# A matmul with rotary embedding on one core: which rows of x share a partition, and which queue brings the block pairs

## The chip, the cores and the metric

The kernel runs on one core of one Trainium2 chip. The metric is the device time of one execution in microseconds, the median over several executions.

## The reference

x has 16 images of 512 rows and 768 columns, in fp32. Each row is multiplied by a 768 x 768 weight, and the 768 results, taken as 12 heads of 64, are rotated by cos and sin, which depend on the row's place in its image alone:

```
y = np.matmul(x, weight)                       # (16, 512, 768) @ (768, 768)
y = y.reshape(batch, seq, n_heads, head_dim)   # 12 heads of 64
y1, y2 = y[..., :32], y[..., 32:]
out1 = y1 * cos1 - y2 * sin1                   # cos, sin: (512, 64), by row of the image
out2 = y2 * cos2 + y1 * sin2
out = np.concatenate([out1, out2], axis=-1)    # fp32, (16, 512, 768)
```

## The kernel before

**Tiles and groups.** The 8192 rows are cut into 64 tiles of 128 rows, and four tiles make a group (16 groups, `QB = 4`). Partition p of a tile holds row 4p + r of one image; a group has the same r in four images (`where`, line 192). So all columns of a group use the same cos and sin rows. Two tiles side by side are a pair; group g has pairs (g, 0) and (g, 1). An image row in DRAM has 3 KB.

**A normal tile.** SyncE loads it as fp32 (`load`, line 206, buffers xs). ScalarE casts it to fp16 and brings its columns into another order (`cast`, line 241, buffers xc). TensorE turns it in PSUM (`turn`, and from tile 4 to 60 `turn_rows`, line 261, which turns the two halves of 64 rows at the same time: line 271 in the profile). ScalarE copies the turned tile to SBUF (buffers xt). These copies and casts all run through the helper `copy`, line 190.

**A block pair.** The second pair of groups 5 to 13 and of group 15 (`BLOCKS`) is not turned by TensorE. It comes in four DMAs of 32 partitions, one per quarter of the columns (`load_quarter`, line 214, packets of 768 bytes), so that VectorE's transpose of 32 x 32 blocks (`turn_pair`, line 287, a STREAM_TRANSPOSE at line 299) finishes the turn. Six pairs come from SyncE as fp32 (buffers xb) and are cast by ScalarE (`cast_pair`, line 279, buffers xd). Four pairs (groups 6, 8, 10, 12) come from GpSimd's queue, whose DMA casts them to fp16 on the way (buffers xh), and need no cast on an engine.

**Matmul and rotation.** From tile 4 on, two streams of matmuls run on the two row halves of TensorE, the second 1024 columns behind the first (`walk`, `one`, `both`; line 362). Six PSUM banks hold a group's 3072 result columns, in units of 512 or 1024. For each unit VectorE multiplies the PSUM columns by cos and by sin (`rope`, line 396; one TENSOR_TENSOR at line 419 writes both products), and GpSimd adds the two products, the second with its half heads exchanged (line 445), into buffers ov. They are stored 768 KB at a time (`store`, line 467), mostly from ScalarE's queue. In the last group some adds are made by TensorE and VectorE.

**Order.** Every engine works through its instructions in the order in which the program issues them, and `Flow.do` puts a semaphore wait ahead of an instruction that needs another engine's result. The order is written out by hand in the main loop over tiles i (line 668). At the end of step i it issues, in this order, the turn of tile i + 3 (with ScalarE's copy), then ScalarE's casts up to tile i + 5, then GpSimd's loads and the stores:

```
700  turns(i + 1 + (T_AHEAD if i > QB else 2), 1)           # T_AHEAD = 3
701  casts(i + 1 + (C_AHEAD if i > QB else 4), 1 + i % 2)   # C_AHEAD = 5
702  pool_loads(i + P_AHEAD)
```

`casts` walks over the tiles; at a normal tile it calls `castx` (line 553), at the first tile of a block pair `cast_pair`, and after each it calls `pump` (line 517), which issues the next loads of the list `fetch` as long as buffers are free (NX tiles, NB block pairs).

Of the kernel before, what the change touches and what calls it, by code (L numbers as in the profile page):

```python
# [108 lines left out]
def kernel(  # L109
# [21 lines left out]
    NT = H // (2 * P)  # L131
    SB = S // P
    QB = 4
    NG = B * SB // QB
# [17 lines left out]
    sin_sb = sbuf("sin_sb", [P, SB, D], FP32)  # L152
# [3 lines left out]
    xs_b = [sbuf(f"xs{i}", [P, H], FP32) for i in range(NX)]  # L156
    xb_b = [sbuf(f"xb{i}", [P, 2 * H], FP32) for i in range(NB)]
    xh_b = [sbuf(f"xh{i}", [P, 2 * H], FP16) for i in range(NBH)]
    xc_b = [sbuf(f"xc{i}", [P, H], FP16) for i in range(NC)]
    xd_b = [sbuf(f"xd{i}", [P, 2 * H], FP16) for i in range(NCP)]  # L160
# [32 lines left out]
    def where(i):  # L193
        g, s = divmod(i, QB)
        return QB * (g // SB) + s, g % SB

# [7 lines left out]


    def load(i, e="sp"):
        b, r = where(i)
        k = ring("xs", NX)
        xs[i] = k
        do(e, lambda eng: eng.dma_start(  # L210
            out=xs_b[k], in_=x[b].rearrange("(p r) h -> r p h", r=SB)[r]),
            writes=[f"xs{k}"], dma=f"xs{k}")

    def load_quarter(gh, q):
        g, h = gh
        b, r = where(g * QB + 2 * h)
        e = BLOCKS[gh]
        src = x[b : b + 2].rearrange("b (j a r) (q k) -> r q a (b j) k", r=SB, a=R, q=NQ)
# [5 lines left out]
        dst = buf.rearrange("p (j k) -> p j k", j=2 * NQ)  # L224
        do(e, lambda eng: eng.dma_start(out=dst[ts(q, R)], in_=src[r, q]),  # L225
           writes=[f"{name}q{q}"], dma=name)

# [13 lines left out]
    def cast(i, e):  # L241
        k = xs[i]
        c = ring("xc", NC)
        xc[i] = c
        do(e, copy(e, xc_b[c].rearrange("p (t m e) -> p t m e", t=NT, e=2),
                   xs_b[k].rearrange("p (m t e) -> p t m e", t=NT, e=2)),
           reads=[f"xs{k}"], writes=[f"xc{c}"])

    def turn(i, e):
        c = xc[i]  # L250
        k = ring("pt", 2)
        z = ring("xt", NXT)
        src = xc_b[c].rearrange("p (t m e) -> p t e m", t=NT, e=2)
        pt = pt_b[k].bitcast(FP16)[:, 0:H].rearrange("p (t e m) -> p t e m", t=NT, e=2)
        for t, h in CHUNKS:
            do("pe", lambda eng: eng.transpose(pt[:, t, h, :], src[:, t, h, :], ident),  # L256
               reads=[f"xc{c}", "ident"], writes=[f"pt{k}"], tick=(t, h) == CHUNKS[-1])
        do(e, copy(e, xt_b[z], pt), reads=[f"pt{k}"], writes=[f"xt{z}"])
        xT[i] = (lambda t, h: xt_b[z][:, t, h, :], f"xt{z}")

    def turn_rows(i, e):

        c = xc[i]
        z = ring("xt", NXT)
        src = xc_b[c].rearrange("p (t m e) -> p t e m", t=NT, e=2)
        pts = [pt_b[r].bitcast(FP16)[:, 0 : H // 2].rearrange(
            "p (t e m) -> p t e m", t=NT, e=2) for r in range(2)]
        for t, h in CHUNKS:
            for r in range(2):
                rows = ts(r, HP)  # L270
                do("pe", lambda eng: eng.transpose(  # L271
                    pts[r][:, t, h, :], src[rows, t, h, :], ident[rows, rows]),
                    reads=[f"xc{c}", "ident"], writes=[f"pt{r}"], tick=(t, h) == CHUNKS[-1])
        do(e, copy(e, xt_b[z].rearrange("p t e (r m) -> p r (t e) m", r=2),
                   pt2.bitcast(FP16)[:, :, 0 : H // 2].rearrange("p r (c m) -> p r c m", m=HP)),
           reads=["pt0", "pt1"], writes=[f"xt{z}"])
        xT[i] = (lambda t, h: xt_b[z][:, t, h, :], f"xt{z}")

    def cast_pair(gh, e="act"):
        k = xs[gh]  # L280
        c = ring("xd", NCP)
        xc[gh] = c
        do(e, copy(e, xd_b[c].rearrange("p (t j e) -> p t j e", t=NT, e=2),
                   xb_b[k].rearrange("p (j t e) -> p t j e", t=NT, e=2)),
           reads=[f"xb{k}q{q}" for q in range(NQ)], writes=[f"xd{c}"])

    def turn_pair(gh):
        g, h = gh
        z = ring("xp", NXP)
        dst = xp_b[z].bitcast(FP32)  # L290
        if BLOCKS[gh] == "pool":
            k = xs[gh]
            src = xh_b[k].bitcast(FP32).rearrange("p (j t) -> p t j", t=NT)
            rd = [f"xh{k}q{q}" for q in range(NQ)]
# [4 lines left out]
        do("dve", lambda eng: eng.transpose(out=dst, in_=src), reads=rd, writes=[f"xp{z}"])  # L299
        for s in (0, 1):  # L300
            xT[g * QB + 2 * h + s] = (
                lambda t, e, s=s: v[:, t, e, ts(s, P)], f"xp{z}")

# [92 lines left out]
    def rope(g, u):  # L396
        c0, c1, ps, banks, adder = u
        w, r = c1 - c0, g % SB
        nh = w // D
        whole = 0 < g and (g, c0 // 1536) < (LAST - 4, 1)  # L400
        if adder == "dve":
# [11 lines left out]
        else:  # L413
# [4 lines left out]
            tq, keys = products(home, 512, 0, 256) if adder == "hold" else products(home, w, 0, w)  # L418
        do("dve", lambda eng: eng.tensor_tensor(  # L419
            out=tq.rearrange("p j (h d) -> p j h d", d=D),  # L420
            in0=ps.rearrange("p (h d) -> p h d", d=D)
            .unsqueeze(1).broadcast_to((P, 2, nh, D)),
            in1=csn[:, :, r, :].unsqueeze(2).broadcast_to((P, 2, nh, D)),
            op=MULT), reads=banks + ["csn"], writes=keys)
        if g not in ov_of:
# [41 lines left out]
    def store(g, c0, c1, e):  # L467

        o = ov_of[g]
        b, r = where(g * QB)  # L470
        s0, s1 = c0 // H, -(-c1 // H)
        dst = out.rearrange("b (p r) h -> r p b h", r=SB)[r, :, b + s0 : b + s1]
        src = ov_b[o].rearrange("p (b h) -> p b h", b=QB)[:, s0:s1]
        if (c1 - c0) % H:
# [3 lines left out]
           reads=[f"ov{o}c{c}" for c in range(c0, c1, 64)],  # L478
           dma=f"xs{c0 // 256 % NX}" if (c1 - c0) % H else f"ov{o}_{c0}")

# [8 lines left out]
    for k in order:  # L489
# [4 lines left out]
    do("sp", lambda eng: eng.dma_start(  # L494
        out=csn[:, 0], in_=cos.rearrange("(p r) d -> p r d", r=SB)), writes=["cos"], dma="ov3_0")
    do("sp", lambda eng: eng.dma_start(
        out=sin_sb, in_=sin.rearrange("(p r) d -> p r d", r=SB)), writes=["sin"], dma="ov3_1536")


    fetch, quarters = [], []  # L500
    soon = [p for p in sorted(BLOCKS) if BLOCKS[p] == "sp"]
    for i in range(QB, NTILE):
        if soon and i >= max(2, soon[0][0] - 1) * QB:
            quarters += [(soon[0], q) for q in (0, 2, 1, 3)]
            soon.pop(0)
        if not is_block(i):
            fetch.append(i)
            for _ in range(2 if i == QB * (LAST - 1) else 1):
                if quarters:
                    fetch.append(quarters.pop(0))  # L510
        elif quarters and quarters[0][0] == pair_of(i):
            fetch.append(quarters.pop(0))
    fetched = [0]
    xs_used, xb_used = [0], [0]
    xs_sent, xb_sent = [4], [0]

    def pump():

        while fetched[0] < len(fetch):
            j = fetch[fetched[0]]  # L520
            if isinstance(j, int):
                if xs_sent[0] - xs_used[0] >= NX:
                    return
                load(j)
                xs_sent[0] += 1
            else:
# [26 lines left out]
    def castx(i, e):  # L553
        cast(i, e)
        xs_used[0] += 1

# [21 lines left out]
    for c in CHUNKS[3:5]:  # L578
# [4 lines left out]
    do("dve", lambda eng: eng.tensor_copy(  # L583
        out=csn[:, 1, :, 0:HD], in_=sin_sb[:, :, HD:D]), reads=["sin"], writes=["csn1"])
    do("dve", lambda eng: eng.tensor_scalar_mul(
        out=csn[:, 1, :, HD:D], in0=sin_sb[:, :, 0:HD], scalar1=-1.0),
        reads=["sin", "csn1", "cos"], writes=["csn"])
    assert not quarters
    pump()
# [164 lines left out]
```

## Time and profile before

Three runs took 150.62, 150.62 and 152.17 us, median 150.62. The profiled execution's span, from its first instruction to its last, is 148.2 us; its time outside the span isn't shown by the profile.

| | before |
|---|---|
| span of the profiled execution | 148.2 us |
| HBM read, written | 27.79 MB, 25.17 MB |
| mean transfer rate | 349 GB/s |
| matmuls of the two streams (line 362) | 1296, 124.2 us busy |
| products on VectorE (line 419) | 110 us busy |
| adds on GpSimd (line 445) | 112 us busy |
| ScalarE waiting for turned tiles | 46.3 us |
| DMA issues on GpSimd for block pairs | 16, 591 ns each |

The profile follows one execution. PE is TensorE's matmul, PEld its weight load, DVE is VectorE, ACT ScalarE, POOL GpSimd, SP SyncE. A group of instructions is given as line, engine, operation, output <- input, shapes, count, then busy time and mean ns of one, then the idle time of its engine just before them and who ended it. Buffer numbers are left out of the names: xt is any of the buffers xt0 to xt7.

### The profile page before, as it was taken

Reading aid. Unit: us, or ns where it says so; the run is one execution under the profiler, and the core shown is the slowest. Engines: PE = TensorE matmul, PEld = TensorE weight load, DVE = VectorE, ACT = ScalarE, POOL = GpSimd, SP = SyncE. Lnnn points to the kernel's source line nnn. Section 1 sums busy time; section 2 is a strip of 40 time slices with the busy share of each in tenths; the row PEclk is TensorE's granted clock in tenths of the full one; section 3 lists DMA queues with packets and bytes.
Section 4 is the critical chain, followed back from the end, with each engine's and each line's share of the span. In section 5 each row is a group of like instructions: output and inputs, shape, how many; then the busy total and the mean of one; then the engine's idle time right before and its main releaser. Section 6 shows DMA issues by size and latency. Waiting matters only on the chain.

```text
span 148.2 us, 4422 instructions
## 1 busy us (share of the span) xinstructions
PE 140.8 (95%) x1948; PEld 112.7 (76%) x1948; DVE 126.0 (85%) x99; ACT 79.0 (53%) x94; POOL 121.8 (82%) x73
## 2 busy tenths in 40 slices
PE   6789999999999999999999999999999999999980
PEld 2335578888888888888888888888888888765860
DVE  0335998886988899899989998999989999999991
ACT  3453898777777933557261915375263919931010
POOL 1000396999999998999999999879699999999990
PEclk9999999999999999999999999999999999999999
DMA  3999999999999999999999999999999999998675
GB/s 124 352 395 403 402 406 398 373 379 296 317 366 330 352 353 277 294 408 287 319 355 397 379 323 358 365 408 324 381 365 337 411 409 416 410 408 333 264 297 180
DMA packets 27555, 51.67 MB, mean 349 GB/s; under 512 B 6160, under 2 KB 13072, under 8 KB 27536
## 3 DMA queue, kind: packets, MB, share of 16 engines
q1 hardware_dynamic: 15824, 28.84, 57.0%
q10 hardware_dynamic: 7360, 20.97, 35.9%
q0 software_dynamic: 4352, 1.57, 8.6%
q8 instruction: 15, 0.25, 0.7%
q14 instruction: 4, 0.03, 0.1%
HBM read 27.79 MB, written 25.17 MB: 357 GB/s over the span
## 4 chain that ended last, share of the span: by engine, by line
PE 78%; DVE 12%; DMA 4%; issue 1%; SPq 1%; DVEq 0%
PE py L362 68%; DVE tq L419 8%; PE py L337 5%; PE pt L271 4%; DMA w_raw<-in_weight_dram 4%; DVE w_raw L419 2%; SPq L210 1%; PE pt L256 1%; DVE ov L445 1%; DVE xs L419 1%; SPq L232 1%; DVE w_sb L190 0%; DVEq L57 0%; SPq L749 0%; SPq L119 0%
## 5 line engine op out<-in xcount | busy, mean ns | idle before, releaser
L445 POOL TENSOR_TENSOR ov<-tq 128x512 f32<-128x512 f32 (+3 forms) x35 | 76.8, 2220 | 20.1 <-DVE tq L419 20.1
L362 PE MATMUL py<-w_sb,xt 64*128 64x256 f16 (+1 forms) x864 | 81.5, 323 | 0.0
L419 DVE TENSOR_TENSOR tq<-py,csn 128x1024 f32<-128x1024 f32 (+2 forms) x51 | 74.4, 1496 | 4.6 <-PE py L362 4.5
L362 PEld LDWEIGHTS py<-w_sb,xt 64*128 64x128 f16 x864 | 59.9, 94 | 11.1 <-DVE tq L419 0.4
L190 ACT COPY xt<-pt 128x768 f16<-128x768 f16 x42 | 33.5, 801 | 47.5 <-PE pt L271 46.3
L362 PE MATMUL py<-w_sb,xp 64*128 64x512 f16 (+1 forms) x432 | 42.7, 323 | 0.0
L190 ACT CAST xc<-xs 128x768 f16<-128x768 f32 x44 | 38.8, 911 | 6.9 <-DMA xs<-in_x_dram 6.7
L419 DVE TENSOR_TENSOR w_raw<-py,csn 128x1024 f32<-128x1024 f32 (+1 forms) x22 | 35.3, 1606 | 4.4 <-PE py L362 4.0
L445 POOL TENSOR_TENSOR ov<-w_raw 128x1536 f32<-128x1536 f32 (+2 forms) x15 | 35.4, 2374 | 1.9 <-DVE w_raw L419 1.9
L362 PEld LDWEIGHTS py<-w_sb,xp 64*128 64x128 f16 x432 | 30.7, 94 | 5.0
L337 PE MATMUL py<-w_sb,xt 128*128 128x256 f16 (+1 forms) x102 | 17.0, 317 | 1.4 <-DVE w_sb L190 1.1
L271 PEld LDWEIGHTS pt<-ident,xc 64*128 64x128 f16 x456 | 14.9, 95 | 1.3 <-issue 0.2
L337 PEld LDWEIGHTS py<-w_sb,xt 128*128 128x128 f16 x102 | 9.2, 98 | 7.4 <-DVE w_sb L190 2.7
L271 PE MATMUL pt<-ident,xc 64*128 64x64 f16 x456 | 14.7, 190 | 0.0
L190 ACT CAST xd<-xb 128x1536 f16<-128x1536 f32 x6 | 9.8, 1634 | 0.0
L225 POOL DMA_DIRECT2D xh<-in_x_dram x16 | 9.4, 591 | 0.0
L190 DVE CAST w_sb<-w_raw 128x768 f16<-128x768 f32 x6 | 3.4, 559 | 3.6 <-DMA w_raw<-in_weight_dram 3.6
L299 DVE STREAM_TRANSPOSE xp<-xd 128x768 f32<-128x768 f32 x6 | 5.8, 970 | 0.0
L190 ACT COPY ov<-py 128x256 f32<-128x256 f32 x1 | 0.4, 372 | 10.1 <-POOL ov L445 10.1
L540 PE MATMUL py<-cold 128*128 128x512 f16 x12 | 4.3, 521 | 1.4 <-DVE cold L482 1.4
L190 DVE COPY xt<-pt 128x768 f16<-128x768 f16 x2 | 1.1, 558 | 4.8 <-PE pt L256 4.8
L299 DVE STREAM_TRANSPOSE xp<-xh 128x768 f32<-128x768 f32 x4 | 4.9, 1234 | 0.0
(23 smaller groups left out, 22.6 us busy)
## 6 DMA issues: line engine op xcount, KB each, us to landing
out_dram<-ov ACTq DMA_DIRECT2D x26, 768.0 KB, 9.6
xs<-in_x_dram SPq DMA_DIRECT2D x44, 384.0 KB, 16.4
xb<-in_x_dram SPq DMA_DIRECT2D x24, 192.0 KB, 16.4
out_dram<-ov SPq DMA_DIRECT2D x4, 768.0 KB, 6.2
w_raw<-in_weight_dram SPq DMA_DIRECT2D x6, 384.0 KB, 6.9
xh<-in_x_dram POOLq DMA_DIRECT2D x16, 96.0 KB, 12.1
out_dram<-ov SPq DMA_DIRECT2D x1, 384.0 KB, 2.3
out_dram<-ov ACTq DMA_DIRECT2D x1, 384.0 KB, 2.3
```

The costliest lines, as they stand in the source:

```text
L190: eng.copy(out=o, in_=i_) if e == "act" else eng.tensor_copy(out=o, in_=i_)
L210: do(e, lambda eng: eng.dma_start(out=xs_b[k], in_=x[b].rearrange("(p r) h -> r p h", r=SB)[r]), writes=[f"xs{k}"], dma=f"xs{k}")
L225: do(e, lambda eng: eng.dma_start(out=dst[ts(q, R)], in_=src[r, q]), writes=[f"{name}q{q}"], dma=name)
L232: do(e, lambda eng: eng.dma_start(out=w_raw[:, t, h], in_=wv[t, h]), writes=[f"wr{t}{h}"], dma=f"ov{t}_0" if h else f"xb{t}")
L256: do("pe", lambda eng: eng.transpose(pt[:, t, h, :], src[:, t, h, :], ident), reads=[f"xc{c}", "ident"], writes=[f"pt{k}"], tick=(t, h) == ...
L271: do("pe", lambda eng: eng.transpose(pts[r][:, t, h, :], src[rows, t, h, :], ident[rows, rows]), reads=[f"xc{c}", "ident"], writes=[f"pt{r ...
L299: do("dve", lambda eng: eng.transpose(out=dst, in_=src), reads=rd, writes=[f"xp{z}"])
L337: do("pe", lambda eng: eng.matmul(ps, get(t, h), w_sb[:, t, h, a - s * H : z - s * H], start=start, stop=stop), reads=[key, f"w{t}{h}"], w ...
L362: do("pe", lambda eng: eng.matmul(py[:, a:z], get(t, h)[rows], w_sb[rows, t, h, a - s * H : z - s * H], start=start, stop=not opens and en ...
L419: do("dve", lambda eng: eng.tensor_tensor(out=tq.rearrange("p j (h d) -> p j h d", d=D), in0=ps.rearrange("p (h d) -> p h d", d=D) .unsque ...
L445: do(adder, lambda eng: eng.tensor_tensor(out=ov_b[o][:, ds(c0, w)].rearrange("p (h t d) -> p h t d", t=2, d=HD), in0=tq[:, 0].rearrange(" ...
L540: do("pe", lambda eng: eng.matmul(py[:, ts(b, 512)], cold[:, 0:P], cold, start=True, stop=warmed[0] < WARM - 6), reads=["cold"], writes=[f ...
```

## The change

**Rows.** For the first 12 images (`NEW = 12`) a group is now one image: its tiles are u, v = 0 0, 0 1, 1 0, 1 1, and partition p of a tile holds row 256u + 2p + v. Two neighbouring rows, 6 KB in DRAM, thus lie in one partition of a pair. Groups 12 to 15 take the last four images as before, one (u, v) in four images each.

**Loads and casts.** Buffers xs and xc hold pairs (NX 10 tiles to 6 pairs, NC 5 tiles to 3 pairs). Pairs 0 to 5 and 24 to 31 are still loaded and cast tile by tile (`by_tile`); normal pairs between come by one DMA of 6 KB rows (`load_two`) and are cast by one instruction (`cast_two`), which `castx` issues at the pair's second tile.

**Block pairs.** All ten come from SyncE as fp32 quarters into xb (NB 3 to 4, NBH 3 to 0) and are cast by `cast_pair`; in groups 12, 13 and 15 each quarter is two DMAs. `turn_pair` writes its result in steps of 8 fp32 elements, and the matmuls read xp as weights in steps of 4 fp16 elements instead of 2.

**Rotation.** The first 12 groups have two rows v in one group, so a unit of 1024 columns takes cos and sin of both: csn has four entries (v = 0, 1, 1, 1), the last two copied once by GpSimd at the start (csnx). Units of 512 columns lie in one row.

**Stores.** In the first 12 groups a store writes 6 KB per partition, 768 KB in one piece of DRAM. The order of the main loop, C_AHEAD, T_AHEAD and the units stay as they are.

```diff
     for g in range(5, 14):
-        BLOCKS[g, 1] = "pool" if g % 2 == 0 and g >= 4 else "sp"
+        BLOCKS[g, 1] = "sp"
...
-    NX, NB, NBH, NC, NCP, NXT, NXP, NOV = 10, 3, 3, 5, 2, 8, 4, 4
+    NX, NB, NBH, NC, NCP, NXT, NXP, NOV = 6, 4, 0, 3, 2, 8, 4, 4
...
-    csn = sbuf("csn", [P, 2, SB, D], FP32)
+    csn = sbuf("csn", [P, 2, 2, 4, D], FP32)
...
-        return QB * (g // SB) + s, g % SB
+        return (g, s) if g < NEW else (NEW + s, g - NEW)
...
+    def by_tile(pr):
+        return pr < 6 or pr >= 2 * NEW
...
+    def load_two(pr, e="sp"):
+        b, r = where(2 * pr)
+        k = xs[pr] = ring("xs", NX)
+        do(e, lambda eng: eng.dma_start(
+            out=xs_b[k], in_=x[b].rearrange("(u p v) h -> u p (v h)", p=P, v=2)[r // 2]),
+            writes=[f"xs{k}_0", f"xs{k}_1"], dma=f"xs{k}_0")
...
+        if g < NEW:
+            src = x[b].rearrange("(u a w) (q k) -> u q a w k", u=2, a=R, q=NQ)[r // 2, q]
+            do(e, lambda eng: eng.dma_start(
+                out=buf.rearrange("p (w k) -> p w k", w=2 * NQ)[ts(q, R)], in_=src),
+               writes=[f"{name}q{q}"], dma=name)
+            return
+        for s in range(2):
+            src = x[b + s].rearrange(
+                "(u a j v) (q k) -> u v q a j k", u=2, a=R, v=2, q=NQ)[r // 2, r % 2, q]
+            do(e, lambda eng: eng.dma_start(out=dst[:, s], in_=src),
+               writes=[f"{name}q{q}" if s else f"{name}q{q}s"], dma=name)
...
+    def cast_two(pr, e):
+        k = xs[pr]
+        c = xc[pr] = ring("xc", NC)
         do(e, copy(e, xc_b[c].rearrange("p (t m e) -> p t m e", t=NT, e=2),
                    xs_b[k].rearrange("p (m t e) -> p t m e", t=NT, e=2)),
-           reads=[f"xs{k}"], writes=[f"xc{c}"])
+           reads=[f"xs{k}_0", f"xs{k}_1"], writes=[f"xc{c}_0", f"xc{c}_1"])
...
-        dst = xp_b[z].bitcast(FP32)
+        dst = xp_b[z].bitcast(FP32).rearrange("p (t a w) -> p t w a", t=NT, a=R)
...
-        v = xp_b[z].rearrange("p (t m e) -> p t e m", t=NT, e=2)
+        v = xp_b[z].rearrange("p (t m s e) -> p t e s m", t=NT, s=2, e=2)
...
+        if mixed:
+            make = lambda eng: eng.tensor_tensor(
+                out=tq, in0=ps.unsqueeze(1).broadcast_to((P, 2, w)),
+                in1=csn[:, u].rearrange("p j g d -> p (j g) d")
+                .unsqueeze(2).broadcast_to((P, 8, w // 256, D)), op=MULT)
...
+        if g < NEW:
+            dst = out[g].rearrange("(u p v) h -> u p (v h)", p=P, v=2)[c0 // (2 * H)]
...
     def castx(i, e):
-        cast(i, e)
-        xs_used[0] += 1
+        if by_tile(i // 2):
+            cast(i, e)
+        elif i % 2:
+            cast_two(i // 2, e)
+        xs_used[0] += i % 2
...
+    two = csn.rearrange("p u j g d -> p (u j) g d")
+    do("pool", lambda eng: eng.tensor_copy(
+        out=two[:, :, 2:4], in_=two[:, :, 1:2].broadcast_to((P, 4, 2, D))),
+        reads=["csn"], writes=["csnx"])
```

More of the change, by code (lines that the diff above doesn't have):

```diff
@@ L132 @@
     SB = S // P
+    NEW = B - SB
     QB = 4
@@ L203 @@
     xs, xc, xT = {}, {}, {}
+    def by_tile(pr):
+        return pr < 6 or pr >= 2 * NEW
     def load(i, e="sp"):
         b, r = where(i)
-        k = ring("xs", NX)
-        xs[i] = k
+        pr, h = divmod(i, 2)
+        if h == 0:
+            xs[pr] = ring("xs", NX)
+        k = xs[pr]
         do(e, lambda eng: eng.dma_start(
-            out=xs_b[k], in_=x[b].rearrange("(p r) h -> r p h", r=SB)[r]),
-            writes=[f"xs{k}"], dma=f"xs{k}")
+            out=xs_b[k][:, ts(h, H)],
+            in_=x[b].rearrange("(u p v) h -> u v p h", p=P, v=2)[r // 2, r % 2]),
+            writes=[f"xs{k}_{h}"], dma=f"xs{k}_{h}")
+    def load_two(pr, e="sp"):
[4 more added lines that the diff above has]
+            writes=[f"xs{k}_0", f"xs{k}_1"], dma=f"xs{k}_0")
     def load_quarter(gh, q):
@@ L223, in load_quarter @@
         buf = xh_b[k] if e == "pool" else xb_b[k]
-        dst = buf.rearrange("p (j k) -> p j k", j=2 * NQ)
-        do(e, lambda eng: eng.dma_start(out=dst[ts(q, R)], in_=src[r, q]),
-           writes=[f"{name}q{q}"], dma=name)
+        dst = buf.rearrange("p (j s k) -> p s j k", j=NQ, s=2)[ts(q, R)]
+        if g < NEW:
[9 more added lines that the diff above has]
+               writes=[f"{name}q{q}" if s else f"{name}q{q}s"], dma=name)
     wv = weight.rearrange("(p t e) n -> t e p n", t=NT, e=2)
@@ L241, in cast, with turned_from @@
     def cast(i, e):
-        k = xs[i]
-        c = ring("xc", NC)
-        xc[i] = c
+        pr, h = divmod(i, 2)
+        k = xs[pr]
+        if h == 0:
+            xc[pr] = ring("xc", NC)
+        c = xc[pr]
+        do(e, copy(e, xc_b[c].rearrange("p (t m e) -> p t m e", t=NT, e=2)[:, :, ts(h, P)],
+                   xs_b[k][:, ts(h, H)].rearrange("p (m t e) -> p t m e", t=NT, e=2)),
+           reads=[f"xs{k}_{h}"], writes=[f"xc{c}_{h}"])
+    def cast_two(pr, e):
+        k = xs[pr]
+        c = xc[pr] = ring("xc", NC)
         do(e, copy(e, xc_b[c].rearrange("p (t m e) -> p t m e", t=NT, e=2),
                    xs_b[k].rearrange("p (m t e) -> p t m e", t=NT, e=2)),
-           reads=[f"xs{k}"], writes=[f"xc{c}"])
+           reads=[f"xs{k}_0", f"xs{k}_1"], writes=[f"xc{c}_0", f"xc{c}_1"])
+    def turned_from(i):
+        c, h = xc[i // 2], i % 2
+        return (xc_b[c].rearrange("p (t m e) -> p t e m", t=NT, e=2)[:, :, :, ts(h, P)],
+                f"xc{c}_{h}")
     def turn(i, e):
-        c = xc[i]
+        src, from_ = turned_from(i)
         k = ring("pt", 2)
         z = ring("xt", NXT)
-        src = xc_b[c].rearrange("p (t m e) -> p t e m", t=NT, e=2)
         pt = pt_b[k].bitcast(FP16)[:, 0:H].rearrange("p (t e m) -> p t e m", t=NT, e=2)
@@ L256, in turn @@
             do("pe", lambda eng: eng.transpose(pt[:, t, h, :], src[:, t, h, :], ident),
-               reads=[f"xc{c}", "ident"], writes=[f"pt{k}"], tick=(t, h) == CHUNKS[-1])
+               reads=[from_, "ident"], writes=[f"pt{k}"], tick=(t, h) == CHUNKS[-1])
         do(e, copy(e, xt_b[z], pt), reads=[f"pt{k}"], writes=[f"xt{z}"])
@@ L272, in turn_rows @@
                     pts[r][:, t, h, :], src[rows, t, h, :], ident[rows, rows]),
-                    reads=[f"xc{c}", "ident"], writes=[f"pt{r}"], tick=(t, h) == CHUNKS[-1])
+                    reads=[from_, "ident"], writes=[f"pt{r}"], tick=(t, h) == CHUNKS[-1])
         do(e, copy(e, xt_b[z].rearrange("p t e (r m) -> p r (t e) m", r=2),
@@ L284, in cast_pair @@
                    xb_b[k].rearrange("p (j t e) -> p t j e", t=NT, e=2)),
-           reads=[f"xb{k}q{q}" for q in range(NQ)], writes=[f"xd{c}"])
+           reads=[f"xb{k}q{q}{o}" for q in range(NQ) for o in ("", "s")], writes=[f"xd{c}"])
     def turn_pair(gh):
@@ L293, in turn_pair @@
             src = xh_b[k].bitcast(FP32).rearrange("p (j t) -> p t j", t=NT)
-            rd = [f"xh{k}q{q}" for q in range(NQ)]
+            rd = [f"xh{k}q{q}{o}" for q in range(NQ) for o in ("", "s")]
         else:
@@ L301, in turn_pair @@
             xT[g * QB + 2 * h + s] = (
[L302 removed]
+                lambda t, e, s=s: v[:, t, e, s], f"xp{z}")
     def units(g):
@@ L397, in rope @@
         c0, c1, ps, banks, adder = u
-        w, r = c1 - c0, g % SB
+        w = c1 - c0
         nh = w // D
+        if g >= NEW:
+            u, v = divmod(g - NEW, 2)
+        else:
+            u, v = c0 // 1536, 0
+        mixed = g < NEW and w > 512
         whole = 0 < g and (g, c0 // 1536) < (LAST - 4, 1)
@@ L418, in rope @@
             tq, keys = products(home, 512, 0, 256) if adder == "hold" else products(home, w, 0, w)
[L419 to L424, printed above, removed]
+        if mixed:
[3 more added lines that the diff above has]
+                .unsqueeze(2).broadcast_to((P, 8, w // 256, D)), op=MULT)
+        else:
+            make = lambda eng: eng.tensor_tensor(
+                out=tq.rearrange("p j (h d) -> p j h d", d=D),
+                in0=ps.rearrange("p (h d) -> p h d", d=D)
+                .unsqueeze(1).broadcast_to((P, 2, nh, D)),
+                in1=csn[:, u, :, v, :].unsqueeze(2).broadcast_to((P, 2, nh, D)), op=MULT)
+        do("dve", make, reads=banks + ["csnx" if mixed else "csn"], writes=keys)
         if g not in ov_of:
@@ L469, in store @@
         o = ov_of[g]
-        b, r = where(g * QB)
+        if g < NEW:
+            dst = out[g].rearrange("(u p v) h -> u p (v h)", p=P, v=2)[c0 // (2 * H)]
+            do(e, lambda eng: eng.dma_start(out=dst, in_=ov_b[o][:, c0:c1]),
+               reads=[f"ov{o}c{c}" for c in range(c0, c1, 64)], dma=f"ov{o}_{c0}")
+            return
         s0, s1 = c0 // H, -(-c1 // H)
-        dst = out.rearrange("b (p r) h -> r p b h", r=SB)[r, :, b + s0 : b + s1]
+        u, v = divmod(g - NEW, 2)
+        dst = out.rearrange("b (u p v) h -> u v p b h", p=P, v=2)[u, v, :, NEW + s0 : NEW + s1]
         src = ov_b[o].rearrange("p (b h) -> p b h", b=QB)[:, s0:s1]
@@ L494 @@
     do("sp", lambda eng: eng.dma_start(
-        out=csn[:, 0], in_=cos.rearrange("(p r) d -> p r d", r=SB)), writes=["cos"], dma="ov3_0")
+        out=csn[:, :, 0, 0:2].rearrange("p u v d -> p u (v d)"),
+        in_=cos.rearrange("(u p v) d -> p u (v d)", p=P, v=2)), writes=["cos"], dma="ov3_0")
     do("sp", lambda eng: eng.dma_start(
-        out=sin_sb, in_=sin.rearrange("(p r) d -> p r d", r=SB)), writes=["sin"], dma="ov3_1536")
+        out=sin_sb.rearrange("p u v d -> p u (v d)"),
+        in_=sin.rearrange("(u p v) d -> p u (v d)", p=P, v=2)), writes=["sin"], dma="ov3_1536")
     fetch, quarters = [], []
     soon = [p for p in sorted(BLOCKS) if BLOCKS[p] == "sp"]
-    for i in range(QB, NTILE):
-        if soon and i >= max(2, soon[0][0] - 1) * QB:
+    for pr in range(2, NTILE // 2):
+        if soon and 2 * pr >= max(2, soon[0][0] - 1) * QB:
             quarters += [(soon[0], q) for q in (0, 2, 1, 3)]
             soon.pop(0)
-        if not is_block(i):
-            fetch.append(i)
-            for _ in range(2 if i == QB * (LAST - 1) else 1):
+        for i in (2 * pr, 2 * pr + 1):
+            if is_block(i):
+                if quarters and quarters[0][0] == pair_of(i):
+                    fetch.append(quarters.pop(0))
+                continue
+            if by_tile(pr):
+                fetch.append(i)
+            elif i % 2 == 0:
+                fetch.append(("two", pr))
+                continue
+            for _ in range(2 if not by_tile(pr) or i == QB * (LAST - 1) else 1):
                 if quarters:
                     fetch.append(quarters.pop(0))
-        elif quarters and quarters[0][0] == pair_of(i):
-            fetch.append(quarters.pop(0))
     fetched = [0]
     xs_used, xb_used = [0], [0]
-    xs_sent, xb_sent = [4], [0]
+    xs_sent, xb_sent = [2], [0]
     def pump():
@@ L520, in pump @@
             j = fetch[fetched[0]]
[L521 to L525, printed above, removed]
+            if isinstance(j, int) or j[0] == "two":
+                if isinstance(j, tuple) or j % 2 == 0:
+                    if xs_sent[0] - xs_used[0] >= NX:
+                        return
+                    xs_sent[0] += 1
+                if isinstance(j, tuple):
+                    load_two(j[1])
+                else:
+                    load(j)
             else:
```

16 lines of the change are left out of this document (7 added, 9 removed).

## The prediction

> **What bounds the kernel now.** I read the page first: busy shares, slices, chain, groups.
>
> ```profile
> PE 140.8 (95%) x1948; PEld 112.7 (76%) x1948; DVE 126.0 (85%) x99; ACT 79.0 (53%) x94; POOL 121.8 (82%) x73
> ...
> PE 78%; DVE 12%; DMA 4%; issue 1%; SPq 1%; DVEq 0%
> ...
> L190 ACT CAST xc<-xs 128x768 f16<-128x768 f32 x44 | 38.8, 911 | 6.9 <-DMA xs<-in_x_dram 6.7
> ...
> L190 ACT CAST xd<-xb 128x1536 f16<-128x1536 f32 x6 | 9.8, 1634 | 0.0
> ...
> L299 DVE STREAM_TRANSPOSE xp<-xd 128x768 f32<-128x768 f32 x6 | 5.8, 970 | 0.0
> ...
> L299 DVE STREAM_TRANSPOSE xp<-xh 128x768 f32<-128x768 f32 x4 | 4.9, 1234 | 0.0
> ```
>
> TensorE is the bound, though ScalarE idles nearly half the time. Next the chain of waits in order of time: from 18.1 to 125.8 us it holds nothing but TensorE, so a microsecond lost there is a microsecond at the end; from 125.86 it is mostly VectorE's last products. Then busy time by stage, one row per group of four tiles with one block pair (columns: stretch, its length, then busy us of PE, PEld, DVE, ACT, POOL, the clock, DMA share, GB/s):
>
> ```profile
> 59.85:68.00 8.15, 8.15 (x125) 7.00 (x122) 7.89 (x5) 4.53 (x6) 8.14 (x6) 1.00 1.08 360
> 68.00:76.15 8.15, 8.15 (x125) 7.00 (x122) 7.71 (x5) 3.33 (x5) 7.89 (x4) 1.00 1.16 309
> ...
> 84.30:92.45 8.15, 8.15 (x125) 7.00 (x122) 7.62 (x5) 3.31 (x5) 7.91 (x4) 1.00 1.15 339
> ```
>
> Every group takes TensorE 8.15 us with no idle, at granted clock 1.00, whatever ScalarE, GpSimd and the DMA do beside it. VectorE has 0.26 to 0.54 us to spare per group. Last, the timelines of ScalarE and of TensorE at tile 12 (start us, us, instruction, idle before it). Counting ScalarE's copies from the start, the one at 29.32 is of tile 11, the one at 31.44 of tile 12:
>
> ```profile
> 27.89 0.91 ACT L190 CAST xc<-xs 128x768 f16<-128x768 f32 x1
> 29.32 0.80 ACT L190 COPY xt<-pt 128x768 f16<-128x768 f16 x1 [0.52 <-PE pt L271]
> 30.01 0.90 ACT L190 CAST xc<-xs 128x768 f16<-128x768 f32 x1
> 31.44 0.80 ACT L190 COPY xt<-pt 128x768 f16<-128x768 f16 x1 [0.54 <-PE pt L271]
> ```
>
> ```profile
> 28.88 0.36 PE L271 MATMUL pt<-ident,xc 64*128 64x64 f16 x11
> 29.05 0.27 PE L362 MATMUL py<-w_sb,xt 64*128 64x256 f16 x1
> 29.07 0.19 PE L271 MATMUL pt<-ident,xc 64*128 64x64 f16 x1
> 29.10 2.11 PE L362 MATMUL py<-w_sb,xt 64*128 64x512 f16 x24
> 31.00 0.36 PE L271 MATMUL pt<-ident,xc 64*128 64x64 f16 x11
> ```
>
> TensorE turns a tile every 2.12 us: tile 11 at 28.88, tile 12 at 31.00. ScalarE follows each turn with its copy and then a cast. The loop's order makes that the cast of the tile two further on: at 27.89 tile 12, at 30.01 tile 13.
>
> **The change part by part.** *Pair casts* (the term that decides). Tiles 12 to 47 outside block pairs are cast in twos, by the call that before cast the odd tile. For tiles 12 and 13 nothing now runs at 27.89, and at 30.01, behind the copy of tile 11, stands one cast of 1536 elements. Its duration is the xd row's, the same shape and access: 1.63 us, so it ends at 31.64. Before, tile 12's cast ended at 28.80, 2.2 us ahead of its turn at 31.00; now TensorE, which works in order, waits with all matmuls behind it. A turn's first weight load has begun 0.05 us after the cast that it waited for (cast to 11.52, load at 11.57) and takes 95 ns itself, so the turn starts at about 31.78: 0.78 us lost. It recurs where the tile before the pair is turned by TensorE in the step before: pairs (12,13), (14,15), (16,17), (18,19) and (20,21). From (24,25) on a block pair stands in front, no copy holds the cast back (one begins at 51.35 and its turn comes at 56.15), and 1.63 us hide in 3 us of idle ScalarE. Sum: 5 x 0.78 = 3.9 us, all in the all-TensorE part of the chain. Eleven pair casts instead of 22 single ones save ScalarE 11 x (2 x 0.91 - 1.63) = 2.1 us, worth nothing on an idle engine.
>
> *Four more block pairs through ScalarE*: 4 x 1.63 = 6.5 us, hidden in the 3.3 to 4.5 of 8.15 us in the rows above; without that cover they would cost the 6.5. Order: such a cast stands where the xd casts of the other groups stand (65.44, 81.74), with one copy behind it, which started 0.1 late there and stopped nothing.
>
> *Block transposes.* The four that read xh in steps of 12 bytes (1.23 us) become ones that read xd (0.97), but all ten now write in steps of 32 bytes, which no row shows. Lower bound 0.97: 4 x 0.26 = 1.06 us off VectorE, worth nothing in groups where TensorE is late. Upper bound twice the row, 1.94. I take 1.23, the only strided row. Up to 0.97 + 0.54 = 1.51 a group still fits in 8.15 us. The last one (124.95, just ahead of the chain's passage to VectorE at 125.86) is on the path: 0.26 us, taken as 0.3.
>
> The Trainium skill (SBUF — State Buffer, note on cachelines under Door 1) says that striding is free up to four fp32 or eight 16-bit values and costs beyond. By that rule the 12-byte read should be free, yet its row is 27% longer than the contiguous one, so the trace disagrees there; the 32-byte write would be penalised by an amount that the page doesn't state, which is the half-speed rival below.
>
> *Weight loads* of xp step by 8 bytes instead of 4. Loads from xt (2 bytes) and xp (4) both take 94 ns, so I take nothing; the other end, doubled loads longer than the 64x256 matmuls' share, would cost some 10 us (432 loads x 94 ns over two row halves = 20 us, half of it hidden).
>
> *GpSimd* loses 16 DMA issues of 591 ns, 9.4 us; no wait of another engine for it lies in the chain before the tail: nothing gained. It gains one copy of 512 elements (csnx), which holds the second product. It may start at 14.90; the first product runs from 14.93 to 16.16. Between 0.30 (its 128-element cast) and 1.28 us (its 512-element add) it ends by 16.2: taken as 0, at most 0.1. The product with csnx has the same 2048 elements (2.28 us): 0.
>
> *DMA.* Longer rows, no cast DMAs, SBUF bytes up by 1.57 MB. ScalarE's four waits for x (6.7 us) are all over by 15.3 us, so faster transfers buy nothing. SyncE issues 28 more quarter DMAs and 11 fewer tile loads, 17 x 0.43 = 7.3 us, and itself waits 29 us for ScalarE to free buffers. Cover: six pairs and four block buffers hold loads some three groups (24 us) ahead, against 16.4 us to landing. Without it a group would wait up to 16 us.
>
> Sum: +3.9 + 0.3 = +4.2 on a span of 148.2, 152.4. The median of the runs shown is 150.62, 2.4 over the span; with that the forecast is **154.8**.
>
> **The rivals.** *Not slower: the lost time is repaid.* The chain ends in VectorE, so if VectorE sets the end, early TensorE waits cost nothing. It decides if VectorE has work stored when TensorE stalls. Against: before 125.86 VectorE waits for TensorE in every group. Time: 150.6, with the transpose term 150.9. *Strided writes run at half speed*: above 1.51 us VectorE becomes the bound in nine groups. At 1.70: 9 x 0.19 + 0.73 = 2.4, 157.2; at 1.94: 9 x 0.43 + 0.97 = 4.8, 159.6. For it: the xh row, where a smaller step already costs. *The traffic was the brake*: without GpSimd's DMAs and with 6 KB rows all runs smoother. At most the 1.06 us of the transposes and some tenths, 149.3; against it, 8.15 us in groups with and without GpSimd's issues. *Slow weight loads*: 160 to 165.
>
> **How the numbers follow.** Forecast 0.62 (153.4 to 155.4: five waits of 0.55 to 0.85 us, and up to 0.53 for transposes of 1.5 us); strided writes 0.15; repaid 0.13; brake 0.07; weight loads or late transfers 0.03. 1% is about what a measurement of this kernel can tell from no change. The range takes the forecast whole, the strided case up to 1.72 us and the repaid case's upper half: 151.0 to 157.5. Faster by over 1% needs more than the profile offers: 0.06. Within 1%: 0.14. Slower: 0.80.
>
> **What would show it.** In the changed profile TensorE's idle names ScalarE's xc five times, 0.7 to 0.8 us each, before 50 us, and each such cast starts right behind a copy; groups with block pairs keep 8.15 us; the transposes' row gives the strided write. I am wrong if those turns start on time, if VectorE appears in the chain before 125 us, or if a group's period changes.

## The result and the profile after

The changed kernel took 156.73 to 160.22 us in four runs, median 158.65, against 150.62; the ratio is 1.043, 95% interval 1.033 to 1.053, which on 150.62 us is 157.1. The profile is of the longest of its four runs (span 158.4 us), and the ratio leaves the two longest out, so the late waits below may be longer in the profile than in the runs behind the ratio.

The page after: busy shares, the chain by engine, and the groups that answer to those shown of before.

```profile
PE 144.3 (91%) x1948; PEld 108.7 (69%) x1948; DVE 130.2 (82%) x99; ACT 84.5 (53%) x87; POOL 113.5 (72%) x58
...
PE 39%; SPq 23%; DMA 13%; ACT 11%; DVE 9%; issue 3%; ACTq 0%; DVEq 0%
...
L191 ACT CAST xc<-xs 128x768 f16<-128x768 f32 (+1 forms) x33 | 37.5, 1143 | 17.9 <-DMA xs<-in_x_dram 17.7
...
L396 PEld LDWEIGHTS py<-w_sb,xp 64*128 64x128 f16 x432 | 31.6, 110 | 5.0
...
L333 DVE STREAM_TRANSPOSE xp<-xd 128x768 f32<-128x768 f32 x10 | 15.8, 1584 | 3.8 <-ACT xd L191 3.8
L191 ACT CAST xd<-xb 128x1536 f16<-128x1536 f32 x10 | 16.4, 1639 | 1.7 <-DMA xb<-in_x_dram 1.7
```

The chain is no longer TensorE's alone: SyncE's queue (SPq) and the loads have 36% of it. ScalarE's casts of normal tiles now wait 17.7 us for x instead of 6.7. Two losses can be placed. The first is the forecast one, in TensorE's timeline (start us, us, instruction, idle before it):

```profile
29.73 0.34 PE L305 MATMUL pt<-ident,xc 64*128 64x64 f16 x10
...
32.54 0.35 PE L305 MATMUL pt<-ident,xc 64*128 64x64 f16 x12 [0.45 <-ACT xc L191]
...
34.68 0.34 PE L305 MATMUL pt<-ident,xc 64*128 64x64 f16 x12
...
37.43 0.35 PE L305 MATMUL pt<-ident,xc 64*128 64x64 f16 x12 [0.47 <-ACT xc L191]
```

From the turn of tile 11 to that of tile 12 pass 2.81 us instead of 2.12, then 2.14 to tile 13, then 2.75 to tile 14: every pair cast holds its turn back. ScalarE's copies of tiles 12, 14, 16, 18 and 20 start 1.52, 2.16, 2.82, 3.47 and 4.12 us later than before: 0.87 at the start, and 0.65 for each of five pairs.

The second was not part of the forecast's sum. ScalarE's timeline near the end, and the chain that leads there (start us, us, what):

```profile
126.88 0.92 ACT L191 CAST xc<-xs 128x768 f16<-128x768 f32 x1 [3.83 <-DMA xs<-in_x_dram]
...
130.72 0.87 ACT L191 CAST xc<-xs 128x768 f16<-128x768 f32 x1 [2.23 <-DMA xs<-in_x_dram]
131.97 1.54 ACT L191 CAST xd<-xb 128x1536 f16<-128x1536 f32 x1 [0.38 <-DMA xb<-in_x_dram]
133.42 0.79 ACT L191 COPY xt<-pt 128x768 f16<-128x768 f16 x1
```

```profile
119.30 0.56 SPq L247
119.90 12.05 DMA xb<-in_x_dram
131.97 1.54 ACT xd L191
133.51 0.71 ACT xt L191
134.26 0.35 PE pt L305 x12
134.62 3.59 PE py L396 x18
```

The last quarter of the last block pair is issued at 119.9 and lands at 131.95 us; before, it was issued at 105.0. Its cast starts 8.7 us later than before (131.97 against 123.30). Behind that cast in ScalarE's queue stands the copy of a turned tile, and TensorE's next turn waits for the copy 3.4 us in the trace. The 18 matmuls after it are on the chain for 3.59 us; before, 17 at this place took 1.94 us. The line of the chain before, and the issues of quarters before and after (duration ns min/median/max, first and last start us):

```profile
123.84 1.94 PE py L362 x17
```

```profile
L225 SPq DMA_DIRECT2D xb<-in_x_dram x24: 432/1228/5867, 19.8 to 105.0; - x24
...
L247 SPq DMA_DIRECT2D xb<-in_x_dram x24: 560/856/2696, 88.0 to 119.9; - x24
```

### The profile page after: what moved, and what is told of

It is laid out like the page before. It is cut to its first block, busy times and chain, and to the rows that moved or that the text cites. A ratio compares the mean times of both kernels' runs of the same rounds, so it can differ in the third digit from the quotient of the medians.

```text
span 158.4 us, 4418 instructions
## 1 busy us (share of the span) xinstructions
PE 144.3 (91%) x1948; PEld 108.7 (69%) x1948; DVE 130.2 (82%) x99; ACT 84.5 (53%) x87; POOL 113.5 (72%) x58
## 4 chain that ended last, share of the span: by engine, by line
PE 39%; SPq 23%; DMA 13%; ACT 11%; DVE 9%; issue 3%; ACTq 0%; DVEq 0%
PE py L396 34%; SPq L247 14%; DMA xb<-in_x_dram 8%; SPq L216 6%; DMA xs<-in_x_dram 6%; ACT xc L191 5%; DVE tq L464 5%; PE pt L305 4%; ACT xt L191 3%; DVE w_raw L464 2%; ACT xd L191 2%; SPq L254 2%; PE py L371 1%; DVE xs L464 1%; PE pt L291 1%
## 5 line engine op out<-in xcount | busy, mean ns | idle before, releaser
L396 PE MATMUL py<-w_sb,xt 64*128 64x256 f16 (+1 forms) x864 | 82.9, 327 | 0.0
L396 PEld LDWEIGHTS py<-w_sb,xt 64*128 64x128 f16 x864 | 55.6, 95 | 16.9 <-issue 1.1
L191 ACT CAST xc<-xs 128x768 f16<-128x768 f32 (+1 forms) x33 | 37.5, 1143 | 17.9 <-DMA xs<-in_x_dram 17.7
L464 DVE TENSOR_TENSOR tq<-py,csn 128x1024 f32<-128x1024 f32 (+2 forms) x35 | 38.9, 1139 | 3.6 <-PE py L396 3.6
L459 DVE TENSOR_TENSOR tq<-py,csn 128x2048 f32<-128x2048 f32 x16 | 36.5, 2281 | 2.8 <-PE py L396 2.8
L396 PEld LDWEIGHTS py<-w_sb,xp 64*128 64x128 f16 x432 | 31.6, 110 | 5.0
L459 DVE TENSOR_TENSOR w_raw<-py,csn 128x2048 f32<-128x2048 f32 x8 | 18.3, 2284 | 2.2 <-PE py L396 2.1
L333 DVE STREAM_TRANSPOSE xp<-xd 128x768 f32<-128x768 f32 x10 | 15.8, 1584 | 3.8 <-ACT xd L191 3.8
L464 DVE TENSOR_TENSOR w_raw<-py,csn 128x1024 f32<-128x1024 f32 x14 | 17.1, 1221 | 1.6 <-PE py L396 1.3
L191 ACT CAST xd<-xb 128x1536 f16<-128x1536 f32 x10 | 16.4, 1639 | 1.7 <-DMA xb<-in_x_dram 1.7
L191 ACT COPY ov<-py 128x256 f32<-128x256 f32 x1 | 0.4, 372 | 10.1 <-PE py L500 10.1
```

The lines of the kernel that those rows point to most:

```text
L191: eng.copy(out=o, in_=i_) if e == "act" else eng.tensor_copy(out=o, in_=i_)
L396: do("pe", lambda eng: eng.matmul(py[:, a:z], get(t, h)[rows], w_sb[rows, t, h, a - s * H : z - s * H], start=start, stop=not opens and en ...
L459: make = lambda eng: eng.tensor_tensor(out=tq, in0=ps.unsqueeze(1).broadcast_to((P, 2, w)), in1=csn[:, u].rearrange("p j g d -> p (j g) d" ...
L464: make = lambda eng: eng.tensor_tensor(out=tq.rearrange("p j (h d) -> p j h d", d=D), in0=ps.rearrange("p (h d) -> p h d", d=D) .unsqueeze ...
```

## The experiments

All ratios are against the kernel before, run beside each kernel on the same chip. The table has the medians and when the cast of the last block pair starts in the profiled execution (before: 123.3). In e4, e9, e10a, e10b, e124 and e14w the block pairs hold their rows in another order than the reference, and these six leave out putting them right: they are there for their times alone.

| kernel | median us | ratio, 95% interval | last block cast, us |
|---|---|---|---|
| e1_tile_casts | 159.43 | 1.057, 1.047 to 1.066 | 131.0 |
| e2_pool_pairs | 155.15 | 1.028, 1.017 to 1.039 | 127.5 |
| e4_contiguous_transpose | 159.43 | 1.042, 1.027 to 1.058 | 132.6 |
| e6_before_all_sync | 161.11 | 1.065, 1.054 to 1.077 | 132.9 |
| e5_fp32_on_gpsimd_queue | 155.45 | 1.025, 1.014 to 1.036 | 127.2 |
| e9_block_pairs_whole_rows | 150.74 | 1.002, 0.996 to 1.007 | 124.3 |
| e12_pool_pairs_tile_casts | 153.33 | 1.019, 1.012 to 1.027 | 125.8 |
| e124_also_contiguous_transpose | 152.93 | 1.014, 1.005 to 1.023 | 125.5 |
| e10a_short_packets_all_partitions | 150.24 | 0.996, 0.992 to 1.000 | 123.7 |
| e10b_long_packets_quarter_partitions | 150.03 | 0.998, 0.995 to 1.002 | 123.4 |
| e13_last_pair_fetched_earlier | 151.76 | 1.007, 1.004 to 1.010 | 124.0 |
| e14w_new_rows_block_pairs_whole_rows | 151.79 | 1.008, 1.004 to 1.011 | 124.1 |

**Undoing one part each.** Tile casts in the changed kernel:

```diff
-        if by_tile(i // 2):
-            cast(i, e)
-        elif i % 2:
-            cast_two(i // 2, e)
+        cast(i, e)
```

> The changed kernel, but every normal tile is cast by its own instruction again, at its own place in ScalarE's order, out of the pair buffers; loads, stores and block pairs stay changed. If the pair casts cost TensorE 5 waits of 0.65 us that are lost for good, this is 3.2 us faster than the changed kernel (about 157.1): 153.9, and the turns of tiles 12 to 20 come every 2.12 us. If the loads of the last groups come late because the transfers are the bound, TensorE only reaches that wait sooner: 156 to 157. If both hold in part, between them.

The turns came every 2.12 us again (copies of tiles 11 and 12 at 29.89 and 32.01), yet the time did not fall: 159.43 us. The last block cast stayed near 131 us. So in the changed kernel as it is, the five waits cost nothing: what they take, TensorE would spend waiting for the last loads.

Block pairs on GpSimd's queue again:

```diff
-        BLOCKS[g, 1] = "sp"
+        BLOCKS[g, 1] = "pool" if g % 2 == 0 else "sp"
...
-    NX, NB, NBH, NC, NCP, NXT, NXP, NOV = 6, 4, 0, 3, 2, 8, 4, 4
+    NX, NB, NBH, NC, NCP, NXT, NXP, NOV = 6, 3, 3, 3, 2, 8, 4, 4
```

> The changed kernel, but the four block pairs of groups 6, 8, 10 and 12 come from GpSimd's queue as fp16 again (three xh buffers, three xb buffers instead of four); the new rows, pair loads and pair casts stay. If bringing all ten pairs from SyncE makes the last loads late, ScalarE no longer waits for x or xb after 100 us and the time falls by 2.5 to 3.5 us to 153.6 to 154.6; the five waits behind the pair casts stay. If the 6 KB rows make the loads late, the waits after 100 us stay and the time is 156.5 to 157.5. The transposes of xh, with strided reads and strided writes, could be slower than 1.58 us and take back up to 1 us.

155.15 us; ScalarE's waits for x are back to 7.7 us, all at the start, and TensorE's chain has only the five waits again. The xh transposes, with steps on both sides, took 1.60 us, no longer than the others.

Contiguous transposes:

```diff
-        dst = xp_b[z].bitcast(FP32).rearrange("p (t a w) -> p t w a", t=NT, a=R)
+        dst = xp_b[z].bitcast(FP32)
```

> The changed kernel, but the block transposes write their result contiguously; the rows of a block pair then come out in another order. Contiguous writes should take 0.97 us instead of 1.58. If the strided write is what costs, VectorE has 0.6 us per group to spare again and the time falls by 1 to 2 us, to 155 to 156. If 1.58 us still fits beside TensorE and late loads set the end, it stays within 0.5 us of 157.1.

The transposes fell to 969 ns, the time did not: 1.042 against 1.043. The last block cast still starts late, at 132.6.

**One part alone, on the kernel before.**

```diff
-        BLOCKS[g, 1] = "pool" if g % 2 == 0 and g >= 4 else "sp"
+        BLOCKS[g, 1] = "sp"
...
-    NX, NB, NBH, NC, NCP, NXT, NXP, NOV = 10, 3, 3, 5, 2, 8, 4, 4
+    NX, NB, NBH, NC, NCP, NXT, NXP, NOV = 10, 4, 0, 5, 2, 8, 4, 4
```

> The kernel before with its old rows, tile loads and tile casts, but all ten block pairs as fp32 quarters from SyncE, cast by ScalarE (four xb buffers, no xh). If SyncE's queue alone cannot bring the loads in time, ScalarE waits for x after 100 us and the time is 152 to 154. If the new rows are needed for that, it is 150.3 to 151: ScalarE has room for the four casts and the transposes read xd at 0.97 us.

161.11 us: this one edit alone costs more than the whole change. From the table of waits (engine, line, waited for: us in total, times, longest us); before, the first row had 6.7 us and the other two weren't there:

```profile
ACT xc L190 <- DMA xs<-in_x_dram: 21.2, 10, 3.2
...
ACT xd L190 <- DMA xb<-in_x_dram: 8.3, 4, 3.0
...
DVE xp L299 <- ACT xd L190: 6.5, 2, 5.6
```

**What in the SyncE quarters is slow.** A third queue with the full bytes (in short: xh buffers in fp32, and `cast_pair` and `xd` for all pairs):

```diff
-    xh_b = [sbuf(f"xh{i}", [P, 2 * H], FP16) for i in range(NBH)]
+    xh_b = [sbuf(f"xh{i}", [P, 2 * H], FP32) for i in range(NBH)]
```

> The kernel before, but the four block pairs on GpSimd's queue come as fp32 (three fp32 buffers) and are cast by ScalarE: the bytes and engine work of e6_before_all_sync, with a third queue. If it is the third queue that brings the last loads in time, ScalarE does not wait for x after 20 us and the time is 150.3 to 151.5. If it is the halved bytes that the casting transfers write to SBUF, the last loads land near 130 us as in e6_before_all_sync and the time is 157 to 161.

In between: 155.45 us (153.18 to 157.28), 29.0 us of waits for x. Neither answer holds alone; the trace also shows that GpSimd's queue sent these bytes in packets of 3072 and 4608 bytes, so it is not the same transfer on another queue, and what the queue alone does stays open.

Then the shape of the transfer, on e6_before_all_sync. Whole rows:

```diff
-        do(e, lambda eng: eng.dma_start(out=dst[ts(q, R)], in_=src[r, q]),
+        rows = x[b + q % 2].rearrange("(p r) h -> r p h", r=SB)[r]
+        cut = ts(q // 2, H // 2)
+        do(e, lambda eng: eng.dma_start(out=buf[:, ts(q, H // 2)], in_=rows[:, cut]),
```

> e6_before_all_sync with the 40 block DMAs of SyncE replaced by DMAs of the same 192 KB over all 128 partitions, in packets of 1536 bytes instead of 768 over 32 partitions; the block pairs then hold rows in another order. If the short packets into a quarter of the partitions are what SyncE's queue cannot sustain, the last loads land before 120 us and the time falls from 161 to 150.3 to 153. If the bytes, or the number of queues, set the rate, it stays above 157.

150.74 us: the same bytes, queue, buffers and number of DMAs, and the whole loss is gone. The edit changes two things, the packets' length (768 to 1536 bytes) and the partitions (32 to 128). Two kernels split it, the first with 768-byte packets over 128 partitions, the second, below the dots, with 6 KB rows into 32 partitions:

```diff
+        rows = x[b + q % 2].rearrange("(p r) (c d k) -> r d p c k", r=SB, c=2, d=2)[r, q // 2]
+        part = buf[:, ts(q, H // 2)].rearrange("p (c k) -> p c k", c=2)
+        do(e, lambda eng: eng.dma_start(out=part, in_=rows),
...
+        rows = x[b + q % 2].rearrange("(z a v) h -> z a (v h)", a=R, v=2)[2 * r + q // 2]
+        do(e, lambda eng: eng.dma_start(out=buf[ts(q, R)], in_=rows),
```

> e6_before_all_sync with block DMAs of the same 192 KB and the same 768-byte packets, but over all 128 partitions (the block pairs hold rows in another order). If the short packets are what makes the loads late, it stays near 161 (above 156). If it is that each quarter writes into 32 partitions only, it falls to 150.3 to 152, as e9_block_pairs_whole_rows did.

> e6_before_all_sync with block DMAs of the same 192 KB into the same 32 partitions each, but in rows of 6 KB instead of 768 bytes (the block pairs hold other rows). If the packets' length is the cause, it falls to 150.3 to 152; if the 32 partitions are, it stays above 156. Together with e10a, values between show how the two share.

150.24 and 150.03 us. Each fell as if the other property were the cause: short packets alone cost nothing in the time, 32 partitions alone cost nothing, and of the four shapes only the one with both makes the loads late. How far apart the packets lie in DRAM is not it alone: e6 takes the pieces that go to one partition from rows 128 apart, the changed kernel from neighbouring rows, and both lose. Not separated is how many packets go into one partition one behind the other: eight in e6, two in e10a. The transfer rows of the two pages, e6_before_all_sync first (packets, MB, share of 16 engines), show the size of it:

```profile
span 159.7 us, 4426 instructions
...
q1 hardware_dynamic: 20176, 31.99, 62.6%
q10 hardware_dynamic: 7360, 20.97, 33.8%
```

```profile
span 148.5 us, 4426 instructions
...
q1 hardware_dynamic: 20176, 31.99, 58.2%
q10 hardware_dynamic: 7360, 20.97, 35.8%
```

The same packets and bytes on SyncE's queue (q1) took 0.626 x 159.7 = 100 us of the 16 engines, against 0.582 x 148.5 = 86 us over all partitions. Single 768-byte packets took 45.7 ns in the mean against 36.6; and the 3072-byte packets of the normal tiles, the same in both kernels, took 142 against 126, which is the larger half of the difference (7.5 of 14 us).

How much of x comes in the middle of the run orders all these kernels. By the rows of the DMA queues from 20 to 100 us, a stretch in which TensorE has no idle time in e6 or e1, SyncE's queue and GpSimd's brought (GpSimd's casting DMAs counted twice, since they write half the bytes that they read):

| kernels | MB of x, 20 to 100 us | late loads |
|---|---|---|
| e6; the changed kernel, e4, e1 | 15.4; 15.8 to 15.9 | yes |
| e5 | 16.45 | yes |
| before, e12, e124, e13, e2 | 17.1, 17.1, 17.2, 17.3, 17.6 | only e12 and e124, the last pair |
| e10b, e10a, e9, e14w | 18.2, 18.9, 19.1, 19.3 | no |

Against the kernel before, packet times alone don't explain e6. Its four pairs on GpSimd's queue took 8.6% of 148.2 = 12.7 us of the 16 engines; as 768-byte packets they take 4096 x 45.7 ns / 16 = 11.7 us. What is lower is the DMA share of this stretch (the packets' times, over 1 where packets overlap), 1.05 against 1.10, and the normal tiles' packets took 142 ns against 135. Whether the third queue or the halved bytes made the difference isn't separated by any run here.

**Both losses undone.**

> The changed kernel with both undone: even block pairs from GpSimd's queue and tile casts; rows, pair loads and 6 KB stores stay. If the five waits behind the pair casts cost 0.65 us each once the loads come in time, this is 3.2 us under e2_pool_pairs (155.2): 151.5 to 152.3. If the loads become late again when TensorE goes faster, it stays above 154.

153.33 us. The cast of the last block pair again waited for its quarters and started late (125.8), so VectorE waited 1.1 us for it.

> e12_pool_pairs_tile_casts with block transposes that write contiguously, so that the rows of block pairs come out in another order. With the loads in time the strided write (1.58 against 0.97 us) should show: 0.6 us of the last transpose and up to 0.07 us in nine groups, together 0.6 to 1.3 us less than e12. If VectorE's slack hides it, no difference above 0.2 us.

152.93 us; the intervals overlap, so the strided write is not told from noise here. Then the last pair's quarters were fetched ahead of tile 56:

```diff
-        if soon and 2 * pr >= max(2, soon[0][0] - 1) * QB:
+        if soon and 2 * pr >= max(2, soon[0][0] - (3 if soon[0][0] == LAST else 1)) * QB:
...
-            for _ in range(2 if not by_tile(pr) or i == QB * (LAST - 1) else 1):
+            for _ in range(2):
```

> e12_pool_pairs_tile_casts with the quarters of the last block pair (group 15) fetched ahead of tile 56 instead of behind it. In e12 they landed at 125.8 us and VectorE's transposes waited for them. If that late landing is what is left of the loss, this is 151 to 152, against 153.3. If the strided transposes and the rows are the rest, it stays within 0.5 us of e12.

151.76 us. And e1_tile_casts with block DMAs over all partitions, as in e9:

```diff
+        rows = x[b + (q % 2 if g >= NEW else 0)].rearrange("(u p v) h -> u p v h", p=P, v=2)[
+            r // 2, :, (q % 2 if g < NEW else r % 2)]
+        do(e, lambda eng: eng.dma_start(
+            out=buf[:, ts(q, H // 2)], in_=rows[:, ts(q // 2, H // 2)]),
```

> e1_tile_casts (all loads from SyncE, tile casts) with the block DMAs over all 128 partitions in packets of 1536 bytes; the block pairs then hold rows in another order. If the quarters are the whole loss left in e1 (159.4), this comes to 150.5 to 152: new rows, pair loads and 6 KB stores cost next to nothing, and the strided transposes up to 1 us. If the rows themselves cost something, it stays above 153.

151.79 us, against 159.43 for e1: the quarters were its whole loss but 1.1 us. By two different ways the rows, pair loads, 6 KB stores and strided transposes together come to 1.007 and 1.008 of before. No version that leaves the rows in their order beat the kernel before.

## Why the prediction was right in its direction, and where it was wrong

**Pair casts.** The mechanism, the five pairs and the place were as forecast; each wait was 0.65 us, not 0.78. The sum gave the turn's first weight load another 95 ns, and took the cast to end 1.63 us after its start: the trace has 1.60, and the turn's matmul 0.06 us behind it. Their price, too, shows once the loads are in time: e2_pool_pairs (five waits, no late load) takes 155.15 us, e13 (no waits, no late load) 151.76, 3.4 us (3.1 by the ratios) for 5 x 0.65 = 3.3. But in the changed kernel these are not what sets the end: e1 removed them and gained nothing.

**Late transfers: the step that failed.** The sum held that faster transfers buy nothing, since all waits for x were over by 15.3 us, and that six pairs and four block buffers give cover of three groups. It never asked whether slower transfers would use the cover up, and left that case 0.03 together with the weight loads. Its own rows had the warning: the DMA share of the groups was 1.08 to 1.16, so the transfer engines had no free time left for a slower shape. Twenty block tiles instead of twelve now came through SyncE's queue in 768-byte packets over 32 partitions, and in the middle of the run x came in at 15.8 MB in 80 us instead of 17.1. SyncE issued its last block quarter at 119.9 us instead of 105.0, and the last groups waited. That alone costs some 10 us on the kernel before (e6, 0.065 x 150.3). In e6's table of waits TensorE's matmuls wait for ScalarE's copies 5.2 us once and 3.3 us in two further waits; with the 1.9 us of slower clock behind them (last section) that comes to 10.4. The price the text gave for lost cover, up to 16 us for one group, is not what any one wait reached. The forecast, 154.8, is 2.3 under the 157.1 of the ratio, which lies near the top of the range of 151.0 to 157.5, and the median of all four runs, 158.65, lies above it. That the forecast came so near is luck: one loss stood in the place of the other.

**Four more casts on ScalarE, 28 more DMAs on SyncE.** Zero holds as far as it was tested: e9 and e10a do the four casts, with 16 more DMAs on SyncE, at 1.002 and 0.996.

**Transposes.** The strided write was taken as 1.23 us and took 1.58, just over the 1.51 at which a group would still fit. VectorE is then busy all of a group, and TensorE still keeps its 8.15 us, as the busy times by stage of e13 show (columns as in the prediction):

```profile
54.00:62.15 8.15, 8.15 (x123) 7.19 (x120) 8.15 (x6) 3.22 (x4) 6.81 (x3) 1.00 1.16 290
62.15:70.30 8.15, 8.15 (x123) 7.16 (x120) 8.15 (x6) 4.68 (x5) 8.14 (x7) 1.00 1.06 365
```

What is left of the cost is the last transpose, 0.6 us longer (1.61 against 0.98); it would be part of the 1.1 us that e13 and e14w are over before. The other half isn't explained. On the cacheline rule of the Trainium skill (SBUF — State Buffer, Door 1): the 32-byte write does cost, 63% (1584 against 970 ns), as it says without an amount; but a 4-value step of fp16, which it calls free, made a weight load 110 ns instead of 94; the groups kept their 8.15 us.

**csnx.** Right: GpSimd's copy took 0.61 us and was over at 16.45; the second product started at 16.95, right behind the first.

**The rivals.** "Repaid" was wrong as a story of the tail, and yet its statement holds for a reason it didn't name: the early waits cost nothing when something later than they sets the end. Strided writes at half speed did not happen (1.58 us, not 1.94); their two times, 157.2 and 159.6, also counted the last transpose's 0.3 us twice. Traffic was no brake before the change (e9 brought 19.1 MB of x where the kernel before brought 17.1, and took the same time), and became one by it.

The same page of the Trainium skill (SBUF — State Buffer, Door 1) says that 32 partitions reach half of the ports. The landing times don't show it by themselves: e10b's blocks of 32 partitions took 15.1 us where e9's and e10a's of 128 took 7.5 and 8.5, but so did e10b's normal tiles over all 128 partitions (15.7 us, against 10.0 and 10.1). In the total time e10b lost nothing, so the rule alone doesn't explain the loss. Why short packets and few partitions only cost together stays open.

## What to carry to other kernels

Where the transfer engines are busy all the time, the cover of a load is not a number of buffers but how long the rate lasts: compare the bytes that arrive over the whole stage with those that are needed before calling a load hidden. A new transfer shape needs its rate measured beside the other transfers; here its packets slowed the others' too. Merging two instructions into one also merges their due times; look at who waits for the first half. And a loss that is seen in the trace need not be in the time: undo it, and see whether the next one takes its place.

## What was unexpected in the hardware

A wait of TensorE can cost more than its length, for the granted clock was lower behind it. In the clock records of the traces, the changed kernel, after 3.4 us of waiting, has 3.41 us at 0.5 of full speed; e1_tile_casts and e6_before_all_sync, with waits of 5.5 and 5.2 us, have 6.83 us, the first 2.6 to 3.0 us of it still in the wait. The kernel before has no such stretch ahead of its end. The 18 matmuls behind the wait took 3.59, 3.63 and 3.83 us in the three, against 1.94 for 17 before, so each lost over 1.5 us more. The busy times of e1 show it (granted clock in the third place from the right):

```profile
130.00:134.00 4.00, 0.67 (x15) 0.60 (x17) 1.39 (x1) 3.83 (x5) 0.00 (x0) 0.54 1.03 411
134.00:138.00 4.00, 4.00 (x43) 2.40 (x40) 3.52 (x4) 1.86 (x4) 2.59 (x3) 0.61 0.94 382
138.00:142.00 4.00, 4.00 (x49) 2.62 (x45) 3.15 (x3) 2.11 (x3) 2.92 (x3) 1.00 0.60 237
```

The lengths agree with the Trainium skill (TensorE: Matmul & The Clock Gate, What's actually happening), which gives windows of 3413 ns and half speed after an idle one. The 3.41 us ahead of the changed kernel's slow stretch were not idle to the end, though: the turn at 134.26 began 0.5 us before it.

The start of a run isn't the same in all kernels: ScalarE's copy of tile 11 began at 29.32 to 29.43 us in four traces with the old rows (before, e6, e5, e10b), at 29.71 and 30.32 in two others with them (e10a, e9), and at 29.70 to 30.25 in all with the new rows. With one trace for each kernel, it stays open whether the 0.87 us at the changed kernel's start belongs to the change.
